# Gradient clipping by the global norm: squares shared by two engines, a split last load and a cut first store

One Trainium2 chip, one core. The metric is the device time of one execution in microseconds (us); where a median is given it is over the runs of one kernel on one chip.

## The reference

```python
# grad: 512 x 4096 float32, max_norm = 1.0
norm = np.sqrt(np.sum(grad ** 2))
scale = min(1.0, max_norm / (norm + 1e-8))
return (grad * scale).astype(np.float32)
```

8.39 MB are read and 8.39 MB written. No element can be scaled before all have been squared and summed.

## The kernel before

The tensor is cut into eight chunks of 128 partitions x 2048 columns (1 MB each, rows of 8 KB), which all stay in SBUF.

```python
ones = small_pool.tile([P, P], fp32, name="ones")
nc.vector.memset(ones, 1.0)
# ...
for i in range(nch):
    # ... ch = data_pool.tile([P, F], ...)
    nc.sync.dma_start(out=ch, in_=gin[i])
for i in range(nch):
    nc.vector.tensor_tensor_reduce(out=sq, in0=chunks[i], in1=chunks[i],   # scale, scalar cut
        op0=mybir.AluOpType.mult, op1=mybir.AluOpType.add, accum_out=acc[:, i : i + 1])
nc.vector.tensor_reduce(out=s, in_=acc, axis=mybir.AxisListType.X, op=mybir.AluOpType.add)
nc.tensor.matmul(tot_psum, ones, s, start=True, stop=True)      # sum over partitions
nc.scalar.activation(out=nrm, in_=tot_psum, func=mybir.ActivationFunctionType.Sqrt)
# nrm_eps = nrm + 1e-8;  inv = reciprocal(nrm_eps);  scl = min(inv * max_norm, 1)   (VectorE)
for i in range(nch):
    nc.vector.tensor_scalar(out=chunks[i], in0=chunks[i], scalar1=scl, scalar2=None,
                            op0=mybir.AluOpType.mult)
    nc.sync.dma_start(out=gout[i], in_=chunks[i])
```

## Time and profile before

| Kernel before | value | how to read it |
|---|---|---|
| time | 52.39 us (52.35 to 52.5, 5 runs) | median |
| profiled span | 50.6 us | first to last instruction of the profiled run; some 1.8 us less than the time |
| loads | first byte 1.80, last landing 22.99 | packet and landing records |
| no DMA | 22.5 to 29.2 | the empty slices in the row by slice |
| stores | bytes from 29.23 to 49.41 | 20.18 us |
| tail | 1.17 us | from the last stored byte to the span's end |

The lines of this profile stand in the prediction below. In profile lines DVE is VectorE, ACT ScalarE, PE TensorE (PEld its weight load), POOL GpSimd and SPq the queue of SyncE, which issues the DMA transfers; L47 is line 47 of the kernel. "Landing" is the moment at which a transfer's semaphore reports it complete.

### The profile page before, as it was taken

How to read it: one execution, taken by the hardware profiler on the slowest of the kernel's cores; microseconds unless marked ns; L12 is line 12 of the kernel's file. 1: busy time of each engine (PE TensorE's matmuls, PEld its weight loads, DVE VectorE, ACT ScalarE, POOL GpSimd, SP SyncE). 2: the span in 40 equal slices, each digit the busy share in tenths (PEclk: the TensorE clock that was granted, in tenths of full speed). 3: DMA queues.
4: the chain of work that ended last, by engine and by line, in shares of the span. 5: the costliest groups of instructions: out<-in, count | busy, mean ns of one | idle time of the engine just before them, and what ended most of it. 6: DMA issues, size and time to landing. Idle time of an engine off the chain costs nothing.

```text
span 50.6 us, 112 instructions
## 1 busy us (share of the span) xinstructions
PE 0.6 (1%) x2; PEld 0.5 (1%) x2; DVE 28.9 (57%) x29; ACT 1.5 (3%) x2; POOL 0.2 (0%) x4
## 2 busy tenths in 40 slices
PE   0000000000000000000040000000000000000000
PEld 0000000000000000000030000000000000000000
DVE  1000597989898989898929999999900000000000
ACT  4500000000000000000010000000000000000000
POOL 1000000000000000000000000000000000000000
DMA  0399999999999999950000099999999999999980
GB/s 0 78 395 408 415 434 428 421 441 434 421 428 415 428 421 428 415 227 0 0 0 0 0 415 415 415 415 415 415 415 415 415 415 415 428 421 421 434 369 0
DMA packets 2304, 16.78 MB, mean 332 GB/s; under 512 B 256, under 2 KB 256, under 8 KB 256
## 3 DMA queue, kind: packets, MB, share of 16 engines
q1 hardware_dynamic: 2304, 16.78, 79.9%
HBM read 8.39 MB, written 8.39 MB: 332 GB/s over the span
## 4 chain that ended last, share of the span: by engine, by line
DMA 37%; DVE 23%; SPq 6%; DVEq 2%; issue 1%; PE 1%; ACT 0%
DMA ch<-in_grad_dram 37%; DVE ch L86 17%; SPq L44 6%; DVE sq L47 5%; DVEq L124 2%; PE tot L63 1%; ACT nrm L66 0%; DVE inv L74 0%; DVE s L59 0%; DVE nrm_eps L70 0%; DVE scl L76 0%; DVEq L47 0%; DVE acc L47 0%
## 5 line engine op out<-in xcount | busy, mean ns | idle before, releaser
L47 DVE CUSTOM_DVE_ANT_0 sq<-ch 128x2048 f32<-128x2048 f32 x8 | 18.3, 2292 | 6.0 <-DMA ch<-in_grad_dram 6.0
L86 DVE TENSOR_SCALAR ch<-ch,scl 128x2048 f32<-128x2048 f32 x8 | 9.7, 1282 | 0.0
L66 ACT ACT_TABLE_LOAD x1 | 1.3, 1283 | 0.7 <-PEq L110 0.7
L63 PE MATMUL tot<-s,ones 128*128 128x1 f32 x2 | 0.6, 362 | 25.7 <-DVE s L59 25.7
L66 ACT ACTIVATE nrm<-tot 128x1 f32<-128x1 f32 x1 | 0.2, 172 | 24.3 <-PE tot L63 24.3
L63 PEld LDWEIGHTS tot<-s,ones 128*128 128x128 f32 x2 | 0.5, 310 | 25.7 <-DVE s L59 25.7
L47 DVE DVE_READ_ACCUMULATOR2_ANT acc<- 128x1 f32 x8 | 0.7, 83 | 0.0
L70 DVE TENSOR_SCALAR nrm_eps<-nrm 128x1 f32<-128x1 f32 x1 | 0.2, 154 | 0.9 <-ACT nrm L66 0.9
L36 DVE MEMSET ones<- 128x128 f32 x1 | 0.2, 165 | 0.8 <-PEq L110 0.8
L74 DVE RECIPROCAL inv<-nrm_eps 128x1 f32<-128x1 f32 x1 | 0.2, 164 | 0.0
L59 DVE TENSOR_REDUCE s<-acc 128x1 f32<-128x8 f32 x1 | 0.2, 161 | 0.0
L76 DVE TENSOR_SCALAR scl<-inv 128x1 f32<-128x1 f32 x1 | 0.2, 153 | 0.0
L110 POOL MEMSET const-bfloat16-1.0<- 128x1 bf16 x1 | 0.1, 102 | 0.0
L110 POOL MEMSET const-uint8-127<- 128x1 uint8 x1 | 0.1, 102 | 0.0
L110 POOL MEMSET const-float32-1.0<- 128x1 f32 x1 | 0.1, 99 | 0.0
L110 POOL MEMSET const-float32-0.0<- 128x1 f32 x1 | 0.1, 98 | 0.2 <-issue 0.2
## 6 DMA issues: line engine op xcount, KB each, us to landing
ch<-in_grad_dram SPq DMA_DIRECT2D x8, 1024.0 KB, 11.8
out_dram<-ch SPq DMA_DIRECT2D x8, 1024.0 KB, 8.5
```

The lines of the kernel that those rows point to most:

```text
L36: nc.vector.memset(ones, 1.0)
L44: nc.sync.dma_start(out=ch, in_=gin[i])
L47: nc.vector.tensor_tensor_reduce(out=sq, in0=chunks[i], in1=chunks[i], scale=1.0, scalar=0.0, op0=mybir.AluOpType.mult, op1=mybir.AluOpTyp ...
L59: nc.vector.tensor_reduce(out=s, in_=acc, axis=mybir.AxisListType.X, op=mybir.AluOpType.add)
L63: nc.tensor.matmul(tot_psum, ones, s, start=True, stop=True)
L66: nc.scalar.activation(out=nrm, in_=tot_psum, func=mybir.ActivationFunctionType.Sqrt)
L70: nc.vector.tensor_scalar(out=nrm_eps, in0=nrm, scalar1=1.0e-8, scalar2=None, op0=mybir.AluOpType.add)
L74: nc.vector.reciprocal(out=inv, in_=nrm_eps)
L76: nc.vector.tensor_scalar(out=scl, in0=inv, scalar1=float(max_norm), scalar2=1.0, op0=mybir.AluOpType.mult, op1=mybir.AluOpType.min,)
L86: nc.vector.tensor_scalar(out=chunks[i], in0=chunks[i], scalar1=scl, scalar2=None, op0=mybir.AluOpType.mult,)
L110: nc = _bacc.Bacc("TRN2", target_bir_lowering=False, num_devices=1)
L124: with _tile.TileContext(nc) as tc:
```

## The change

Its intent is to shorten the stretch between the last load and the first store: share the squares between VectorE and ScalarE, so that the last chunk's work is small; load the last chunk in two contiguous halves; drop the epsilon step; and store the first chunk in four pieces that grow. The diff, cut to its core (helpers for the three engines shortened, a GpSimd one that nothing calls left out):

```diff
-    ones = small_pool.tile([P, P], fp32, name="ones")
-    nc.vector.memset(ones, 1.0)
+    lin = flat_in[c0:].rearrange("(h p f) -> h p f", p=P, f=H)     # last chunk, H = F // 2
     for i in range(nch):
-        nc.sync.dma_start(out=ch, in_=gin[i])
+        if i == last:
+            nc.sync.dma_start(out=ch[:, 0:H], in_=lin[0])
+            nc.sync.dma_start(out=ch[:, H:F], in_=lin[1])
+        else:
+            nc.sync.dma_start(out=ch, in_=gin[i])
+    nc.gpsimd.memset(ones, 1.0)
+    nc.gpsimd.memset(acc, 0.0)                                      # 16 columns
+    nc.scalar.activation(out=warm, in_=ones[:, 0:1], func=...Sqrt)
+    for i in range(nch - 1):
+        if i in (0, 2, 4):
+            sq_accum_vector(chunks[i])        # tensor_tensor_reduce, as before
+        else:
+            sq_accum_act(chunks[i])           # activation Square with accum_out
+    sq_accum_vector(lc[:, 0:H])
+    sq_accum_act(lc[:, H : H + 544])
+    sq_accum_vector(lc[:, H + 544 : F])
...
-    # sqrt; + 1e-8; reciprocal; * max_norm and min 1
+    # sqrt(tot / max_norm**2); reciprocal; min 1
...
+    cuts = [0, 256, 640, 1216, F]
+    for a, b in zip(cuts, cuts[1:]):
+        scale_and_store("dve", chunks[0][:, a:b], gout[0][:, a:b])
+    for i in range(1, nch - 1):
+        scale_and_store("dve", chunks[i], gout[i])
+    for h in range(2):
+        scale_and_store("dve", lc[:, h * H : (h + 1) * H], lout[h])
```

More of the change, by code (lines that the diff above doesn't have):

```diff
@@ L20 @@
     P = nc.NUM_PARTITIONS
+    mn = float(max_norm)
     flat_in = grad.flatten()
@@ L33 @@
     psum_pool = ctx.enter_context(tc.tile_pool(name="psum", bufs=1, space=bass.MemoryType.PSUM))
-    ones = small_pool.tile([P, P], fp32, name="ones")
-    nc.vector.memset(ones, 1.0)
-    acc = small_pool.tile([P, nch], fp32, name="acc")
-    sq = small_pool.tile([P, F], fp32, name="sq")
     chunks = []
+    last = nch - 1
+    H = F // 2
+    c0 = last * P * F
+    lin = flat_in[c0:].rearrange("(h p f) -> h p f", p=P, f=H)
+    lout = flat_out[c0:].rearrange("(h p f) -> h p f", p=P, f=H)
     for i in range(nch):
@@ L43 @@
         chunks.append(ch)
-        nc.sync.dma_start(out=ch, in_=gin[i])
-    for i in range(nch):
+        if i == last:
[3 more added lines that the diff above has]
+            nc.sync.dma_start(out=ch, in_=gin[i])
+    ones = small_pool.tile([P, P], fp32, name="ones")
+    nc.gpsimd.memset(ones, 1.0)
+    sq_v = small_pool.tile([P, F], fp32, name="sq_v")
+    sq_a = small_pool.tile([P, F], fp32, name="sq_a")
@@ new lines, with acc_col @@
+    sq_p = small_pool.tile([P, F // 2], fp32, name="sq_p")
+    NACC = 16
+    acc = small_pool.tile([P, NACC], fp32, name="acc")
+    ai = 0
+    def acc_col():
+        nonlocal ai
+        c = acc[:, ai : ai + 1]
+        ai += 1
+        return c
+    nc.gpsimd.memset(acc, 0.0)
+    warm = small_pool.tile([P, 1], fp32, name="warm")
+    nc.scalar.activation(
+        out=warm, in_=ones[:, 0:1], func=mybir.ActivationFunctionType.Sqrt
+    )
+    Square = mybir.ActivationFunctionType.Square
+    add = mybir.AluOpType.add
@@ L47, with sq_accum_vector @@
+    mult = mybir.AluOpType.mult
+    def sq_accum_vector(src):
         nc.vector.tensor_tensor_reduce(
-            out=sq,
-            in0=chunks[i],
-            in1=chunks[i],
+            out=sq_v[:, 0 : src.shape[1]],
+            in0=src,
+            in1=src,
             scale=1.0,
             scalar=0.0,
-            op0=mybir.AluOpType.mult,
-            op1=mybir.AluOpType.add,
-            accum_out=acc[:, i : i + 1],
-        )
+            op0=mult,
+            op1=add,
+            accum_out=acc_col(),
+        )
@@ new lines, in sq_accum_act, with sq_accum_pool @@
+    def sq_accum_act(src):
+        nc.scalar.activation(
+            out=sq_a[:, 0 : src.shape[1]],
+            in_=src,
+            func=Square,
+            accum_out=acc_col(),
+        )
+    def sq_accum_pool(src):
+        w = src.shape[1]
+        nc.gpsimd.tensor_tensor(out=sq_p[:, 0:w], in0=src, in1=src, op=mult)
+        nc.gpsimd.tensor_reduce(
+            out=acc_col(), in_=sq_p[:, 0:w], axis=mybir.AxisListType.X, op=add
+        )
+    for i in range(nch - 1):
[3 more added lines that the diff above has]
+            sq_accum_act(chunks[i])
@@ L58 @@
+    lc = chunks[last]
+    sq_accum_vector(lc[:, 0:H])
+    s0 = H
+    a_w = 544
+    sq_accum_act(lc[:, s0 : s0 + a_w])
+    sq_accum_vector(lc[:, s0 + a_w : F])
     s = small_pool.tile([P, 1], fp32, name="s")
-    nc.vector.tensor_reduce(
-        out=s, in_=acc, axis=mybir.AxisListType.X, op=mybir.AluOpType.add
-    )
+    nc.vector.tensor_reduce(out=s, in_=acc, axis=mybir.AxisListType.X, op=add)
     tot_psum = psum_pool.tile([P, 1], fp32, name="tot")
@@ L65, with scale_and_store @@
     nrm = small_pool.tile([P, 1], fp32, name="nrm")
-    nc.scalar.activation(
-        out=nrm, in_=tot_psum, func=mybir.ActivationFunctionType.Sqrt
-    )
-    nrm_eps = small_pool.tile([P, 1], fp32, name="nrm_eps")
-    nc.vector.tensor_scalar(
-        out=nrm_eps, in0=nrm, scalar1=1.0e-8, scalar2=None, op0=mybir.AluOpType.add
-    )
+    nc.scalar.activation(out=nrm, in_=tot_psum, func=mybir.ActivationFunctionType.Sqrt,
+                         scale=1.0 / (mn * mn))
     inv = small_pool.tile([P, 1], fp32, name="inv")
-    nc.vector.reciprocal(out=inv, in_=nrm_eps)
+    nc.vector.reciprocal(out=inv, in_=nrm)
     scl = small_pool.tile([P, 1], fp32, name="scl")
     nc.vector.tensor_scalar(
-        out=scl,
-        in0=inv,
-        scalar1=float(max_norm),
-        scalar2=1.0,
-        op0=mybir.AluOpType.mult,
-        op1=mybir.AluOpType.min,
-    )
-    for i in range(nch):
-        nc.vector.tensor_scalar(
-            out=chunks[i],
-            in0=chunks[i],
-            scalar1=scl,
-            scalar2=None,
-            op0=mybir.AluOpType.mult,
-        )
-        nc.sync.dma_start(out=gout[i], in_=chunks[i])
+        out=scl, in0=inv, scalar1=1.0, scalar2=None, op0=mybir.AluOpType.min
+    )
+    def scale_and_store(eng, view_sb, view_hbm):
+        if eng == "act":
+            nc.scalar.activation(
+                out=view_sb,
+                in_=view_sb,
+                func=mybir.ActivationFunctionType.Copy,
+                scale=scl,
+            )
+        elif eng == "pool":
+            nc.gpsimd.tensor_scalar(
+                out=view_sb, in0=view_sb, scalar1=scl, scalar2=None, op0=mult
+            )
+        else:
+            nc.vector.tensor_scalar(
+                out=view_sb, in0=view_sb, scalar1=scl, scalar2=None, op0=mult
+            )
+        nc.sync.dma_start(out=view_hbm, in_=view_sb)
+    cuts = [0, 256, 640, 1216, F]
[5 more added lines that the diff above has]
+        scale_and_store("dve", lc[:, h * H : (h + 1) * H], lout[h])
 _INS = ['grad', 'max_norm']
```

## The prediction

> **What bounds the kernel now.** I read the rows by slice first, to see which resource is full when.
>
> ```profile
> DVE  1000597989898989898929999999900000000000
> DMA  0399999999999999950000099999999999999980
> GB/s 0 78 395 408 415 434 428 421 441 434 421 428 415 428 421 428 415 227 0 0 0 0 0 415 415 415 415 415 415 415 415 415 415 415 428 421 421 434 369 0
> ```
>
> Each column is 1.26 us (50.6 us in 40 slices). There are two plateaus of DMA at 400 to 440 GB/s, the loads and the stores, and a hole of five empty slices between them. Every byte must be squared before the first byte can be scaled, so the plateaus cannot overlap, and both run at the same rate whatever the engines do. The hole is what can be shortened. The groups of instructions show whether an engine holds back a plateau:
>
> ```profile
> L47 DVE CUSTOM_DVE_ANT_0 sq<-ch 128x2048 f32<-128x2048 f32 x8 | 18.3, 2292 | 6.0 <-DMA ch<-in_grad_dram 6.0
> L86 DVE TENSOR_SCALAR ch<-ch,scl 128x2048 f32<-128x2048 f32 x8 | 9.7, 1282 | 0.0
> ```
>
> A square takes 2.29 us, and chunks land 2.47 to 2.48 us apart (trace of landings: 20.52 and 22.99 for the last two), so VectorE already keeps up and waits 0.17 to 0.19 us for each chunk. A scaling takes 1.28 us, half of the 2.5 us that a chunk's store takes, so VectorE doesn't hold the stores either. The chain that ended last, in order of time, shows the hole step by step (start, duration, what):
>
> ```profile
> 4.29 18.70 DMA ch<-in_grad_dram
> ...
> 23.12 2.29 DVE sq L47
> 25.41 0.02 DVE acc L47
> 25.43 0.03 issue
> 25.46 0.17 DVE s L59
> 25.63 0.04 issue
> 25.67 0.60 PE tot L63 x2
> ...
> 26.30 0.18 ACT nrm L66
> 26.48 0.02 issue
> 26.50 0.17 DVE nrm_eps L70
> ...
> 26.69 0.17 DVE inv L74
> ...
> 26.89 0.16 DVE scl L76
> 27.05 0.02 issue
> 27.07 1.29 DVE ch L86
> ```
>
> The last load lands at 22.99. From there: 2.47 us to the sum's start at 25.46 (nearly all of it the last square), 1.61 us of short links to the first scaling at 27.07, 1.31 us to the first store's issue at 28.39. The packet records have the first stored bytes at 29.23 (0.84 us after the issue) and the last at 49.41: 20.18 us for 8.39 MB, 416 GB/s. A tail of 1.2 us follows. The waits of the engines say the same: ScalarE idles until the matmul.
>
> ```profile
> ACT nrm L66 <- PE tot L63: 24.3, 1, 24.3
> DVE sq L47 <- DMA ch<-in_grad_dram: 6.0, 8, 4.6
> ```
>
> **What the Trainium skill says.** "VectorE: DVE Perf Modes", section "Side-by-side: where the cycles go for N=2048 bf16", gives about 2293 ns for one element a cycle at 0.96 GHz and 1224 ns for two; its section on mode 2×_2P says that a single-source fp32 operation in SBUF gets two a cycle. The trace has 2292 and 1282 ns, so it agrees on the form. I fit fixed parts to the trace: 2292 − 2048/0.96 = 159 ns for a square, 1282 − 2048/1.92 = 215 ns for a scaling. "ScalarE: Activation LUTs", section "What ACT_TABLE_LOAD costs", gives 1283 ns for the load and 186 ns + 0.833 ns an element for an ACTIVATE with immediates. The trace has 1283 ns for the load and 172 ns for the one ACTIVATE of one element; no ACTIVATE of many elements is in it. "DMA: Bandwidth & Descriptors", section "Why small descriptors are slow (HBM only)", counts about 3 cycles a packet beside one per 32 bytes. The trace has only 8192-byte data packets, median 309 ns, so it cannot test this.
>
> **The change part by part.**
> (1) Squares of chunks 1, 3, 5, 6 move to ScalarE. By the formula one takes 1892 ns (an estimate), under the 2.48 us spacing. Nothing to gain in itself, since VectorE kept up. It does leave both engines free when the last chunk lands.
> (2) The last chunk is loaded in two halves, now contiguous 4 KB rows. The first half should land about 1.24 us earlier, at 21.75, and VectorE starts it at 21.87 (0.12 us after landing, as now). It takes 1024/0.96 + 159 = 1226 ns, to 23.10; the accumulator's read and its signal bring the second start to 23.15. The remaining 480 columns take 500 + 159 = 659 ns, and the sum could start at 23.86. ScalarE takes the other 544 columns: from 23.12, 186 + 453 = 639 ns to 23.76, plus reading its accumulator, which no row shows (VectorE's takes 83 ns); I allow 0.2, so 23.96, and the sum starts at 24.00. The slower of the two counts: 25.46 − 24.00 = 1.46 saved. Smaller load packets may delay the landing by 1.2% of 2.5 us, 0.03. Net 1.43.
> (3) The epsilon add goes (26.50 to 26.69 in the chain): 0.19 saved. Folding 1/max_norm² into the square root is an immediate and costs nothing. The sum over 16 columns instead of 8 costs some 8 ns.
> (4) The warm-up square root moves nothing: the table load already starts at 0.73, long before it is needed. The built program has one table load in both versions. The memset of the ones moves from VectorE to GpSimd, off the path in both.
> (5) The first scaling is cut into 256, 384, 576 and 832 columns. The first piece takes 133 + 215 = 348 ns, and its store issues 0.03 later: 0.375 against 1.31, so 0.94 saved.
> (6) What (5) gives back. Consecutive scalings overlap by 0.085 us, so pieces are ready at 0.35, 0.68, 1.11, 1.68 and chunk 1 at 2.88 us after the first scaling starts. SyncE needs about 0.43 per issue (early stores: 0.35 plus the gap), so issues fall at 0.38, 0.81, 1.24, 1.71 and 2.91. With 0.84 to the first byte and transfers of 0.32, 0.47, 0.71 and 1.03 us at 416 GB/s, the queue runs dry once: piece 1 ends at 1.53 and piece 2 begins at 1.65, 0.12 lost. Then piece 4 ends at 3.86 and chunk 1 is there at 3.75. Small rows: with the skill's 3 cycles, 1, 1.5, 2.25, 3.25 KB rows and the last chunk's 4 KB rows cost 8, 5, 3, 1.7 and 1.2% more than 8 KB rows, which over those transfers is 0.026 + 0.024 + 0.021 + 0.017 + 0.03 = 0.12. Together 0.24 given back.
> Thirteen stores and nine loads share eight DMA semaphores, so some issues wait on an older transfer. The ninth load waits for the first load (landed at 5.6, with some 17 us of loads still queued); the late stores wait for small early ones. Both are hidden.
> Sum: 1.43 + 0.19 + 0.94 − 0.24 = 2.32. 52.39 − 2.32 = 50.07 us.
>
> **The rivals.**
> A, the split is given back: the small stores stream badly (issue or first-byte cost per store), so that the store plateau lengthens by about as much as its start gains. For it: four issues in sequence, rows of 1 to 3 KB, rates no trace shows. Against it: issues took only 0.35 us while the queue was empty, and there are just four. It would leave 1.4 + 0.2, near 50.8.
> B, ScalarE becomes the last link: its ACTIVATE with accumulation costs more than the formula, or its read of the accumulator is long, so the sum waits for it. For it: no such instruction is in this trace. Against it: even 0.5 us more on 544 columns costs only 0.5, giving 50.6. If a whole 2048-column square took over 2.4 us, chunk 6, landing at 20.5, would run into the last chunk and cost more.
> C, the transfers are the bound and the engines' work is hidden anyway: within 2%. For it: both plateaus are at 415 GB/s, 80% of the span. Against it: in the hole the DMA queue does nothing, and every removed link lies in the hole.
> D, better than computed: short ScalarE read, full rate at small rows: 49.7.
>
> **Range and chances.** The terms I trust least are the 1.43 (±0.25) and the 0.24 (0 to 0.8). They give 49.6 to 50.6. For less than 2% the time must stay over 51.34, so more than half of the 2.32 must be lost, which needs A and B together, or the last chunk badly delayed. Faster by over 2%: 0.95; within 2%: 0.045; slower: 0.005.
>
> **What would show it.** Right: the last load still lands near 23.0; the sum starts near 24.0; the first scaling near 25.4; the first store's issue near 25.8; stored bytes flow for some 20.4 us; span about 48.3. The engine to look at in the wait ahead of the sum is ScalarE. Wrong: a last landing over 23.2 (then the split of the load costs), zeros in the GB/s row after the first store (rival A), or ScalarE squares over 2.2 us (rival B).

## The result

The changed kernel takes 50.42 us in the median (50.37 to 50.63, 8 runs) against 52.38 us (52.26 to 52.5, 15 runs of the same rounds). The ratio is 0.9636, with a 95% interval of 0.9622 to 0.9651: faster by 3.6%. Ratios here are the mean time of one kernel's fast runs over that of the other's of the same rounds, so not quite the ratio of the medians quoted. The output is correct.

The rows by slice of the changed kernel (40 slices of 1.22 us) show that ScalarE now works during the loads and that the hole has shrunk: two zeros and a 21 in place of five zeros.

```profile
DVE  0000395029601970009739999999920000000000
ACT  4800003930294019595610000000000000000000
DMA  0589999999999999993000999999999999999970
GB/s 0 88 371 418 411 424 431 431 431 431 425 431 418 424 431 418 384 404 128 0 0 21 336 405 425 431 431 424 411 404 398 411 431 431 431 431 371 414 293 0
```

The chain that ended last, from the second-to-last landing on (start, duration, what):

```profile
21.89 1.17 DVE sq_v L78
23.06 0.07 DVE acc L78
23.13 0.02 issue
23.15 0.66 DVE sq_v L78
...
23.92 0.18 DVE s L117
24.10 0.14 issue
24.24 0.57 PE tot L119 x2
24.81 0.02 issue
24.83 0.18 ACT nrm L121
25.01 0.02 issue
25.04 0.17 DVE inv L124
25.21 0.02 issue
25.23 0.17 DVE scl L126
25.40 0.03 issue
25.42 0.35 DVE ch L143
```

Compare it with the chain in the prediction. The square of 2.29 us behind the last landing is one of 0.66; `nrm_eps` is gone; the first `ch` is 0.35 instead of 1.29. The gap of 0.14 ahead of the matmul was 0.04 before. The groups with shapes kept apart give the durations that the prediction had to assume:

```profile
L90 ACT ACTIVATE sq_a<-ch 128x2048 f32<-128x2048 f32 x4 | 7.6, 1910 | 12.3 <-DMA ch<-in_grad_dram 12.3
L90 ACT ACTIVATION_READ_ACCUMULATOR sq_a<-ch 128x1 f32 x5 | 0.9, 186 | 0.0
L78 DVE CUSTOM_DVE_ANT_0 sq_v<-ch 128x480 f32<-128x480 f32 x1 | 0.7, 658 | 0.0
L90 ACT ACTIVATE sq_a<-ch 128x544 f32<-128x544 f32 x1 | 0.7, 657 | 0.5 <-DMA ch<-in_grad_dram 0.5
L143 DVE TENSOR_SCALAR ch<-ch,scl 128x256 f32<-128x256 f32 x1 | 0.4, 353 | 0.0
```

The whole span now splits into five stretches, read from the chain and the packet records of both traces:

| stretch (us) | before | after | saved | predicted |
|---|---|---|---|---|
| span's start to the sum's start | 25.46 | 23.92 | 1.53 | 1.43 |
| sum's start to the first scaling | 1.62 | 1.50 | 0.12 | 0.19 |
| first scaling to the first stored byte | 2.16 | 1.23 | 0.93 | 0.94 |
| first to last stored byte | 20.18 | 20.61 | −0.44 | −0.24 |
| last stored byte to the span's end | 1.17 | 1.37 | −0.20 | 0 |
| sum | 50.58 | 48.63 | 1.94 | 2.32 |

The last load landed at 22.99 before and 23.01 after, so nothing came from the loads. The gain is 0.38 smaller than predicted: the stores' plateau (0.20), the tail (0.20) and the link to the matmul (0.07) fell short, and the last chunk gained 0.10 more than computed.

### The profile page after: what moved, and what is told of

It reads as the page before. It is cut to its first block, busy times and chain, and to the rows that moved or that the text cites.

```text
span 48.6 us, 135 instructions
## 1 busy us (share of the span) xinstructions
PE 0.6 (1%) x2; PEld 0.5 (1%) x2; DVE 19.5 (40%) x25; ACT 10.4 (21%) x13; POOL 0.5 (1%) x6
## 4 chain that ended last, share of the span: by engine, by line
DMA 36%; DVE 25%; SPq 7%; issue 2%; PE 1%; DVEq 1%; ACT 0%
DMA ch<-in_grad_dram 36%; DVE ch L143 20%; SPq L49 7%; DVE sq_v L78 4%; PE tot L119 1%; DVEq L185 1%; ACT nrm L121 0%; DVE s L117 0%; DVE inv L124 0%; DVE scl L126 0%; DVE acc L78 0%; DVEq L117 0%; DVEq L78 0%
## 5 line engine op out<-in xcount | busy, mean ns | idle before, releaser
L78 DVE CUSTOM_DVE_ANT_0 sq_v<-ch 128x2048 f32<-128x2048 f32 (+2 forms) x5 | 8.8, 1752 | 15.0 <-DMA ch<-in_grad_dram 15.0
L90 ACT ACTIVATE sq_a<-ch 128x2048 f32<-128x2048 f32 (+1 forms) x5 | 8.3, 1659 | 12.9 <-DMA ch<-in_grad_dram 12.9
L143 DVE TENSOR_SCALAR ch<-ch,scl 128x2048 f32<-128x2048 f32 (+5 forms) x12 | 10.2, 926 | 0.0
L90 ACT ACTIVATION_READ_ACCUMULATOR sq_a<-ch 128x1 f32 x5 | 0.9, 186 | 0.0
```

Source lines behind the costliest of these rows:

```text
L78: nc.vector.tensor_tensor_reduce(out=sq_v[:, 0 : src.shape[1]], in0=src, in1=src, scale=1.0, scalar=0.0, op0=mult, op1=add, accum_out=acc_ ...
L90: nc.scalar.activation(out=sq_a[:, 0 : src.shape[1]], in_=src, func=Square, accum_out=acc_col(),)
L143: nc.vector.tensor_scalar(out=view_sb, in0=view_sb, scalar1=scl, scalar2=None, op0=mult)
```

## The experiments

The theory is the prediction's: three separate cuts in the stretch without DMA (last chunk, epsilon, first store), partly given back by the stores. The rivals are A (the first store's split is given back), B (ScalarE is the last link ahead of the sum) and C (the transfers bind, the hole is hidden). Experiments undo one part at a time, then look at the terms that were off. Each was run beside the kernel before on one chip: u_cuts to u_eps on one, dve_last to ones_dve on a second, the last four on a third. Where such a run is compared with the changed kernel's 50.42, it is mostly across chips; the changed kernel itself took 50.42 and 50.49, so a difference of 0.1 needs its trace. The diffs are cut to their core, and a comment in them can stand for several lines.

| run | median (us) | runs | ratio to before | 95% interval |
|---|---|---|---|---|
| changed kernel, first | 50.42 | 8 | 0.9636 | 0.9622 to 0.9651 |
| u_cuts | 50.95 | 4 | 0.973 | 0.971 to 0.975 |
| u_last | 51.92 | 4 | 0.9913 | 0.9894 to 0.9933 |
| u_act | 52.0 | 4 | 0.9932 | 0.9912 to 0.9953 |
| u_eps | 50.63 | 5 | 0.9665 | 0.9646 to 0.9684 |
| dve_last | 51.03 | 4 | 0.9748 | 0.9731 to 0.9765 |
| last_8k | 50.84 | 4 | 0.9704 | 0.969 to 0.9717 |
| rows4k | 51.06 | 4 | 0.9749 | 0.9736 to 0.9762 |
| ones_dve | 50.39 | 5 | 0.9613 | 0.96 to 0.9626 |
| after_again (changed kernel) | 50.49 | 4 | 0.9648 | 0.9633 to 0.9664 |
| ones_again | 50.39 | 4 | 0.9627 | 0.9612 to 0.9642 |
| cuts3 | 50.37 | 4 | 0.9625 | 0.9604 to 0.9646 |
| best | 50.34 | 5 | 0.9621 | 0.9602 to 0.964 |

### The first store whole again

```diff
-    cuts = [0, 256, 640, 1216, F]
+    cuts = [0, F]
```

> The changed kernel with the first chunk scaled and stored whole again (one scaling of 2048 columns, one 1 MB store with 8 KB rows). Theory of the prediction: the first store's issue moves 0.94 us later (from 25.80 to about 26.74), but the dry spell of about 0.1 us and the slow small rows go; with the packet times of the changed kernel's trace (46, 65, 95, 132 ns for 1, 1.5, 2.25, 3.25 KB rows against 309 for 8 KB) those rows cost 0.24 us, so the time rises by 0.94 - 0.1 - 0.24 = 0.6 us, to 51.0. Rival A (the split is given back in the stores): rise of 0.2 or less.

It took 50.95 us, 0.53 more than the changed kernel. The first stored byte came at 27.54, 0.89 later, and the stores' bytes took 20.31 instead of 20.61 us, 0.31 less. So a third of the earlier start is given back; rival A is right in kind, and in size it takes 0.31 of 0.89. The cut is worth 0.5 us.

### The last chunk whole again

```diff
-    # two loads, two halves squared by VectorE / ScalarE + VectorE, two stores
+    nc.sync.dma_start(out=ch, in_=gin[i])        # every chunk
+    sq_accum_vector(lc)
+    scale_and_store("dve", lc, gout[last])
```

> The changed kernel with the last chunk loaded in one piece, squared whole by VectorE and stored whole; chunks 1, 3, 5, 6 stay on ScalarE. Theory: the last square again stands whole behind the last landing, so the sum starts near 25.45 instead of 23.92, and the time rises by 1.5 us less about 0.13 for the last chunk's store rows (8 KB instead of 4 KB), to 51.8. It shows too that ScalarE's share of the squares is worth nothing without the split: apart from the eps step (0.19), the first store (0.6) and small change it would stand near before. Rival C (the queue bounds, the hole is hidden): within 0.3 of the changed kernel.

It took 51.92 us, 1.5 more than the changed kernel: of the whole gain of 1.96 us, 0.46 are left. The timeline of this run shows why (start, duration, engine, line, operation, tiles, idle before it):

```profile
20.51 1.91 ACT L86 ACTIVATE sq_a<-ch 128x2048 f32<-128x2048 f32 x1 [0.48 <-DMA ch<-in_grad_dram]
22.32 0.19 ACT L86 ACTIVATION_READ_ACCUMULATOR sq_a<-ch 128x1 f32 x1
23.02 2.29 DVE L74 CUSTOM_DVE_ANT_0 sq_v<-ch 128x2048 f32<-128x2048 f32 x1 [5.13 <-DMA ch<-in_grad_dram]
25.24 0.08 DVE L74 DVE_READ_ACCUMULATOR2_ANT acc<- 128x1 f32 x1
25.42 0.17 DVE L109 TENSOR_REDUCE s<-acc 128x1 f32<-128x16 f32 x1
```

Half of the squares are on ScalarE, VectorE idles 5.13 us before the last one, and the sum still starts at 25.42, as before. Taking four squares off VectorE moves nothing by itself. (This run keeps the other parts of the change, from which its 0.46 come.) The time returns with the length of the last square, so rival C (the hole is hidden by the transfers) falls.

### Every square on VectorE, the last load still split

```diff
-        if i in (0, 2, 4):
+        if True:
-    sq_accum_act(lc[:, s0 : s0 + a_w])
-    sq_accum_vector(lc[:, s0 + a_w : F])
+    sq_accum_vector(lc[:, H:F])
```

> The changed kernel with every square on VectorE; the last chunk is still loaded in halves and squared by VectorE in two halves of 1024. Theory: chunk 6's square ends at 22.95, so the halves run one after the other to about 25.45 and the early landing of the first half is worth nothing; the sum starts near 25.5 and the time rises by 1.6 us, to 52.0. So moving whole squares to ScalarE is worth nothing by itself but the split is worth nothing without it. Rival (the split of the load alone gives the gain and ScalarE's share only its 0.5): rise of 0.5, to 50.9.

It took 52.0 us and the sum starts at 25.48, as before (25.46), so splitting the load alone is worth nothing either. The timeline shows the queue that forms:

```profile
20.62 2.29 DVE L78 CUSTOM_DVE_ANT_0 sq_v<-ch 128x2048 f32<-128x2048 f32 x1 [0.19 <-DMA ch<-in_grad_dram]
...
22.95 1.22 DVE L78 CUSTOM_DVE_ANT_0 sq_v<-ch 128x1024 f32<-128x1024 f32 x1
24.10 0.08 DVE L78 DVE_READ_ACCUMULATOR2_ANT acc<- 128x1 f32 x1
24.22 1.22 DVE L78 CUSTOM_DVE_ANT_0 sq_v<-ch 128x1024 f32<-128x1024 f32 x1
25.37 0.08 DVE L78 DVE_READ_ACCUMULATOR2_ANT acc<- 128x1 f32 x1
25.48 0.17 DVE L114 TENSOR_REDUCE s<-acc 128x1 f32<-128x16 f32 x1
```

The first half landed at 21.77, but VectorE was busy with chunk 6 until 22.95 and did the two halves one after the other. The split and ScalarE's share each give nothing without the other; together they give 1.5 us. The two undone parts (1.5 and 1.58) therefore do not add up to two gains.

### The last half chunk on VectorE alone

```diff
-    sq_accum_act(lc[:, s0 : s0 + a_w])
-    sq_accum_vector(lc[:, s0 + a_w : F])
+    sq_accum_vector(lc[:, H:F])
```

> The changed kernel with the last half chunk squared by VectorE alone (1024 columns) instead of by ScalarE (544) and VectorE (480). Theory: VectorE ends 1.226 us after 23.15 instead of 0.66, the sum starts 0.5 us later and the time rises by 0.5 us, to 50.9. Rival B (ScalarE with its accumulator read is what the sum waits for): a smaller rise, as 0.3.

It took 51.03 us, 0.6 more. From the last landing to the sum's start it is 1.50 us in this trace (23.21 to 24.71) and 0.92 in the changed kernel's (23.01 to 23.92): 0.59, near the 0.57 by which 1226 ns exceeds 658. So ScalarE's 544 columns are worth nearly the whole of what VectorE is spared, and rival B is not seen: in the changed kernel both engines' last reads end within 0.02 us of each other (ScalarE's at 23.840, VectorE's at 23.821 in the trace).

### The epsilon step back

```diff
+    nc.vector.tensor_scalar(out=nrm_eps, in0=nrm, scalar1=1.0e-8, scalar2=None, op0=add)
-    nc.vector.reciprocal(out=inv, in_=nrm)
+    nc.vector.reciprocal(out=inv, in_=nrm_eps)
```

> The changed kernel with the add of 1e-8 put back between the square root and the reciprocal. Theory: one more dependent VectorE step of 154 ns plus about 40 ns of hand-over on the path: rise of 0.19 us, to 50.6. Rival (hidden behind something): 0.

It took 50.63 us, 0.21 more. The intervals of the two ratios just overlap (0.9646 to 0.9684 and 0.9622 to 0.9651), but the trace shows it: from the sum's start to the first scaling it is 1.69 us here and 1.50 in the changed kernel. So a step of 154 ns on the only chain costs itself and its hand-over, 0.19 in all.

### More rows of 4 KB in the stores

```diff
     for i in range(1, nch - 1):
-        scale_and_store("dve", chunks[i], gout[i])
+        for a, b in ((0, H), (H, F)):
+            scale_and_store("dve", chunks[i][:, a:b], gout[i][:, a:b])
```

> The changed kernel with chunks 1 to 6 scaled and stored in column halves too, so that all but the first chunk's store rows are 4 KB. It measures the disputed cost per packet by itself on six chunks (768 rows of 8 KB become 1536 of 4 KB, 96 more packets on each engine). If a packet costs what the changed kernel's trace says (2 x 162 - 309 = 15 ns each pair): 48 x 15 = 0.72 us more, to 51.1. By the 3 cycles of the skill (1.2% of 15.1 us): 0.18 us more, to 50.6.

It took 51.06 us, 0.64 more. The profiled run took 51.15, 0.73 more: 0.16 is its later last landing (23.17 against 23.01), 0.07 its tail, and the stores' bytes took 21.11 us instead of 20.61, 0.50 more. The queue did not run dry for want of issues: the DMA share over the stores is 1.01, against 1.00 in the changed kernel. (The expectation's "96 more packets" should be 48, as its own sum has it.) The row by slice shows a lower plateau over its whole length:

```profile
GB/s 0 66 358 412 425 425 425 425 425 425 445 431 431 412 425 405 405 412 47 0 0 87 345 407 406 402 408 408 395 415 405 402 405 408 405 408 405 402 285 0
```

From the 407 to the last full slice it stays at 395 to 415, where the changed kernel, on 8 KB rows, has mostly 404 to 431 (with a 398, and a 371 near the last chunk). 0.50 us for 48 more packets on each engine are 10.4 ns for a packet. The same comes from the mean packet durations: 315.5 ns for 8 KB, 163.5 for 4 KB, 134.6, 96.4, 68.0 and 47.9 for the first chunk's four kinds of rows (3.25 to 1 KB). Two of 4 KB are 11.5 ns longer than one of 8 KB; eight of 1 KB are 67 ns longer, 9.6 for each of the seven added. That is three times what the prediction took from the Trainium skill, "DMA: Bandwidth & Descriptors", section "Why small descriptors are slow (HBM only)" (3 cycles against 256: 1.2% for a 4 KB row, an estimate of under 4 ns).

### The last chunk in the old layout

```diff
-            nc.sync.dma_start(out=ch[:, 0:H], in_=lin[0])
-            nc.sync.dma_start(out=ch[:, H:F], in_=lin[1])
+            nc.sync.dma_start(out=ch[:, 0:H], in_=gin[i][:, 0:H])
+            nc.sync.dma_start(out=ch[:, H:F], in_=gin[i][:, H:F])
-    # stored in two halves
+    scale_and_store("dve", lc, gout[last])
```

> The changed kernel with the last chunk in the layout of before: its halves are loaded as column halves (4 KB rows, strided in HBM), and it is scaled and stored whole with 8 KB rows. Theory: two 4 KB packets took 2 x 162 = 324 ns against 309 for one of 8 KB, so the last chunk's store is 0.12 us shorter and the time falls by 0.1 to 0.15 us. By the 3 cycles of the skill: 0.03.

It took 50.84 us: 0.42 slower where I expected 0.1 faster. The stores' bytes did take a little less (20.55 against 20.61). The loss is in the loads, which now fetch every other 4 KB of the chunk, twice. Stretches of this run, then of the changed kernel (us, length, busy time of the five engines, clock, DMA share, GB/s):

```profile
20.00:21.00 1.00, 0.00 (x0) 0.00 (x0) 0.00 (x0) 0.51 (x2) 0.00 (x0) 1.00 0.97 307
21.00:21.50 0.50, 0.00 (x0) 0.00 (x0) 0.00 (x0) 0.50 (x1) 0.00 (x0) 1.00 0.81 287
```

```profile
20.00:21.00 1.00, 0.00 (x0) 0.00 (x0) 0.00 (x0) 0.51 (x2) 0.00 (x0) 1.00 1.03 414
21.00:21.50 0.50, 0.00 (x0) 0.00 (x0) 0.00 (x0) 0.50 (x1) 0.00 (x0) 1.00 1.03 410
```

The strided first half ran at about 300 GB/s, its packets took 193 ns in the mean against 162, and the last landing came at 23.48 instead of 23.01; the second half was normal again (160 ns). So the contiguous layout of the halves is worth 0.4 us of the change, which the prediction had not seen. Why the stride slows this half, the runs do not settle: the column-half stores of the rows4k run are strided as well and took 164 ns.

### The ones set by VectorE, twice

```diff
-    nc.gpsimd.memset(ones, 1.0)
+    nc.vector.memset(ones, 1.0)
```

> The changed kernel with the memset of the ones back on VectorE. The prediction said that this move costs nothing. In the changed kernel's trace the matmul waits for two engines, VectorE and GpSimd, and 0.14 us pass between the sum and the matmul, where 0.04 passed before; a semaphore wait of 51 ns of TensorE stands in that gap. Theory: with the ones from VectorE there is one semaphore to wait for, the gap is 0.05 again and the time falls by 0.09 us, to 50.33. Rival (the prediction's own step 4): no change.

The changed kernel's timeline, then that of the second run of this variant:

```profile
23.92 0.17 DVE L117 TENSOR_REDUCE s<-acc 128x1 f32<-128x16 f32 x1
24.21 0.50 PEld L119 LDWEIGHTS tot<-s,ones 128*128 128x128 f32 x2 [24.21 <-issue]
24.24 0.56 PE L119 MATMUL tot<-s,ones 128*128 128x1 f32 x2 [24.24 <-DVE s L117]
24.83 0.17 ACT L121 ACTIVATE nrm<-tot 128x1 f32<-128x1 f32 x1 [0.99 <-PE tot L119]
```

```profile
24.02 0.17 DVE L117 TENSOR_REDUCE s<-acc 128x1 f32<-128x16 f32 x1
24.24 0.50 PEld L119 LDWEIGHTS tot<-s,ones 128*128 128x128 f32 x2 [24.24 <-DVE s L117]
24.24 0.58 PE L119 MATMUL tot<-s,ones 128*128 128x1 f32 x2 [24.24 <-DVE s L117]
24.86 0.17 ACT L121 ACTIVATE nrm<-tot 128x1 f32<-128x1 f32 x1 [0.93 <-PE tot L119]
```

With the ones from GpSimd, the matmul depends on two engines: a semaphore instruction of TensorE (51 ns) stands between the sum and the weights, and 0.91 us pass from the sum's start to the square root; with the ones from VectorE 0.84. This agrees with the Trainium skill, "Perfetto Trace Analysis", section "Identifying Dependency Chains", which notes that an instruction that waits for several engines may have a separate semaphore instruction put in front of it. In time the first run, 50.39 us, could not be told from the changed kernel on another chip, so I repeated it beside it:

> The changed kernel itself once more, so that the three small variants of this call have it on the same chip: 50.4 us.

> The ones set by VectorE again, beside the changed kernel on one chip. The earlier run's trace has 0.74 us from the sum's end to the square root in the changed kernel and 0.68 here, so theory: 0.06 us faster than the changed kernel, 50.35. Rival: no change.

50.39 against 50.49 us on one chip; the direction and the trace agree, but the intervals of the two ratios overlap (0.9612 to 0.9642 and 0.9633 to 0.9664), so the 0.1 is not shown by time alone.

### Three pieces instead of four, and both small changes together

```diff
-    cuts = [0, 256, 640, 1216, F]
+    cuts = [0, 384, 1024, F]
```

> The changed kernel with the first chunk cut at 384 and 1024 (three pieces) instead of 256, 640, 1216 (four). Theory: the first store issues 0.07 us later, but its transfer (0.53 us) is longer than an issue of 0.45, so the dry spell of about 0.1 us goes, and 24 short-row packets an engine instead of 32, of longer rows, save 0.07: 0.1 us faster than the changed kernel, 50.3. Rival (the first store's start is all that counts): 0.07 slower, 50.5.

50.37 us, 0.12 under the changed kernel on the same chip; the intervals overlap (0.9604 to 0.9646, 0.9633 to 0.9664), so the time alone does not show a gain. The stores' bytes took 20.43 us instead of 20.62 (0.2 less), and the issue of the first store came 0.07 later relative to its scaling, as expected. The tail, though, is 0.07 longer (1.44 against 1.37; the account of the tail below says why). That leaves some 0.05 for the cut; the rest of the difference between the two profiled spans, 0.13, is an earlier last landing (22.92 against 23.06), which the cut does not touch. The first two half microseconds of stores in this run and in the changed kernel (its first run):

```profile
26.60:27.10 0.50, 0.00 (x0) 0.00 (x0) 0.50 (x2) 0.00 (x0) 0.00 (x0) 1.00 0.90 323
27.10:27.60 0.50, 0.00 (x0) 0.00 (x0) 0.50 (x1) 0.00 (x0) 0.00 (x0) 1.00 1.08 398
```

```profile
26.60:27.10 0.50, 0.00 (x0) 0.00 (x0) 0.50 (x2) 0.00 (x0) 0.00 (x0) 1.00 0.77 258
27.10:27.60 0.50, 0.00 (x0) 0.00 (x0) 0.50 (x1) 0.00 (x0) 0.00 (x0) 1.00 0.91 324
```

The lower DMA share of the changed kernel, 0.77 and 0.91, holds the dry spell; with three larger pieces it is 0.90 and 1.08 (packet durations overlap, so a share can pass 1). By its packet records the share falls to 0.29 between 27.00 and 27.25, between the first and the second piece, and what is missing there adds up to 0.11 us; with three pieces there is no such dip.

> Both together, the ones on VectorE and the three pieces. Theory: 0.06 + 0.1 faster than the changed kernel, 50.25. Rival: no faster than the changed kernel.

50.34 us, the lowest median, 0.15 under the changed kernel beside it. The intervals (0.9602 to 0.964, 0.9633 to 0.9664) still overlap a little. It is 3.8% faster than the kernel before; against the changed kernel, that it is no slower is all I claim.

## Why the prediction was right

The time lies within the range, 0.35 us above the point. Step by step:

- What bounds the kernel (two plateaus and the hole between them): right. Each undone link came back in the time nearly one for one (the first store's less what the stores give back).
- Steps 1 and 2, the last chunk: right, 1.53 against 1.43. The 0.10 over is luck as far as the total goes: it hides part of what steps 4 and 6 and the tail lost. VectorE's durations were exact (1226, 658 ns against 1226, 659). ScalarE's ACTIVATE was 657 ns instead of 639. Its accumulator read takes 186 ns, but starts some 94 ns before the ACTIVATE ends, so it adds 92, where 200 were allowed. That "moving squares is nothing in itself" is shown by the run with the last chunk whole, and that the split needs it by the run with all squares on VectorE. The 1.2% for smaller load packets could not be seen (landing +0.02).
- Step 3, epsilon: right, 0.19 computed and 0.19 in the trace (0.21 in the time) when it is put back. The square root with the folded factor took 171 ns against 172, and the sum over 16 columns 169 against 161, the 8 ns computed.
- Step 4, the moved memset "off the path": the step that failed in kind, though small. The memset itself is off the path, but it gave the matmul a second engine to wait for, about 0.07 us by the trace.
- Step 5, the first store: right, 0.93 against 0.94, as its own stretch.
- Step 6, what is given back: right in kind, mis-sized: 0.44 measured against 0.24. The term that failed is the row cost. With the measured packets a 1 KB row takes 47.9 ns where an eighth of an 8 KB packet would be 39.4, and so on: 8.5, 8.8, 7.7 and 6.4 ns more, each for 8 rows an engine, are 0.25 us, and 16 rows of 4 KB at 5.75 ns are 0.09. That makes 0.34 in place of 0.12; the rest, 0.10, is the dry spell, put at 0.12 and 0.11 in the packet records. The step's "thirteen stores" are twelve (4 + 6 + 2), which changes no sum.
- The tail was taken as unchanged and grew by 0.20. In the trace of before, SyncE's last wait is the one for the last landing. In the trace of after, three more semaphore waits follow that one, at 47.70, 47.76 and 47.82, some 62 ns apart, before the closing steps. In both kernels eight semaphores report the transfers in turn; with 21 transfers instead of 16 the last landing comes on one that is not the last waited for. No run was made for this, but the variants have other numbers of transfers and so test it. With three waits behind the last landing (the changed kernel twice, u_cuts, u_act, u_eps, dve_last, both ones runs) the tail is 1.34 to 1.37 us; with four (u_last, last_8k, rows4k, cuts3, best) it is 1.41 to 1.45; with none (before) it is 1.17.

Rival A was a part of the truth (0.31 of 0.89 given back), B and C were not. Of D (49.7) one half came true, the short ScalarE read (92 ns on top), and the other, full rate at small rows, did not.

## What to carry to other kernels

Where a reduction stands between loading and storing, only the work behind the last landing and ahead of the first store counts: make the last piece small and have every engine that can do it idle at that moment, for either half of this alone gives nothing. When cutting a first store, charge each added row (here about 10 ns a packet), and try a first transfer longer than the time of one issue: here the dip in the queue went away with it, though the gain in time is not shown. Look, too, at which landing the program waits for last. After moving even a tiny set-up instruction to another engine, look at what each late instruction now waits for.

## What the Trainium skill lacked or had wrong

- "DMA: Bandwidth & Descriptors", section "Why small descriptors are slow (HBM only)": it counts about 3 cycles a packet, and 32 bytes of descriptor metadata an operation, which the prediction left out. Counted as one more 32-byte step, that makes 4 cycles beside 256, as an estimate 5 ns of the 315 of an 8 KB packet. The runs show about 10 ns for each added store packet between 1 and 8 KB: 47.9 ns for 1 KB, 163.5 for 4 KB, 315.5 for 8 KB in the mean, and 0.50 us for 48 added packets on each engine.
- "ScalarE: Activation LUTs", section "What ACT_TABLE_LOAD costs": its formula gives 639 and 1892 ns; measured 657 and 1910 with an accumulator output. It has no figure for the read of the accumulator: 186 ns, of which 92 come on top.
- "Perfetto Trace Analysis", section "Identifying Dependency Chains": it has the extra semaphore instruction but not its cost: by the timelines the gap ahead of the matmul is 0.15 us with it and 0.05 without.
- No page I read has the loss for a load of alternate 4 KB pieces: about 300 instead of 410 GB/s for half a megabyte, landing 0.47 us later. Nor the cost of a wait that is already fulfilled at the end of SyncE's program: 62 ns each, three of them here.
